# When the norm factors, the last sums of squares and two weight chunks are taken in a hybrid encoder trunk

## The chip, the cores and the metric

The kernel runs on one core of a Trainium2 chip. The metric is device time in microseconds (us), the median of several runs; lower is better. A core has TensorE (PE; its weight loads are PEld), VectorE (DVE), ScalarE (ACT), GpSimd (POOL) and SyncE (SP), which issues most DMAs. Each engine works through its own queue in order, and engines wait for one another at semaphores.

## The reference

Two layers on a sequence of 1024 positions of width 1024, all in float32. Cut to what matters:

```python
def rms_norm(x, g):
    y = x * rsqrt(mean(x * x, axis=-1) + 1e-6)
    return y * g

for layer in range(2):
    if layer == 0:
        x = x + ab_mixer(rms_norm(x, ab_norm), ...)   # mLSTM heads and gated MLP groups
    else:
        x = x + mla_mixer(rms_norm(x, c_norm), ...)   # attention from low-rank latents
    hf = rms_norm(x, ffn_norm[layer])
    x = x + square(relu(hf @ ffn_w1[layer])) @ ffn_w2[layer]   # width 4096 inside
return rms_norm(x, final_norm)
```

`mla_mixer` first projects the normed x to a key-value latent of 256 rows, a rotary key and a query latent of 384 rows, and norms both latents.

## The kernel before

Activations lie feature by feature, 128 features on the partitions and 1024 positions along the columns. Each product is made of three: a float32 operand is split into a high part (a ScalarE cast, `hi`, `wo`, `whi`) and a low part (the rest, a subtraction, mostly on VectorE: `lo`, `wlo`), and high x high, high x low and low x high are added up in PSUM. The norm's gain is multiplied in ahead of a product; the norm's factor, one number for each position, is multiplied in behind it. A factor is made in three moves: `rstd_sums` (L519) puts the sums of squares of a position on TensorE, sixteen small matmuls; `rstd_from` (L526) makes the root of it with twelve small VectorE operations; `spread_parts` (L549) builds two diagonal tiles `dg` on VectorE, and `spread_sums` (L567) lets TensorE spread them over the partitions, four matmuls, which ScalarE copies to `rb`.

**The MLP, first half** (`strassen_up`, L627). The product is done by Strassen's scheme: 16 quads q of output tiles, seven products each, so steps g = 7q + s. A product is 12 matmuls of 512 columns into one of four kinds of PSUM bank, A to D, with two banks each. The order of TensorE, VectorE and ScalarE is written out by hand in the loop over g: after the product of step g come, in this order, the weights' parts of step g+3 (`up.parts`), the sum of weights of step g+4 (`up.combine`), loads, relu and square of the results, a sum of the second product's weights (`sums.step`, stored to HBM), and the evacuation of the bank (`evacuate`). The norm's sums stand behind product 3, the factor in step 4, `dg` in step 5, the spread behind product 6; with it `relu` (L696, which multiplies `rb` in) of quad 0 in step 7 and its squares and stores in step 8. For later quads relu stands in the evacuation itself.

**The MLP, second half** (`strassen_down`, L756). Seven passes of eight steps (n = 8 pi + kp, the pass's product is i = DOWN[pi]); a step is 24 matmuls. In each step `fetch` (L395) starts the next weight chunk: a load by SP into one of two buffers `raw`, the cast on ScalarE, the low part on VectorE; `weights` (L415) takes the oldest one out. So a step works on a chunk that was fetched one step earlier. `di.parts(n + 2)` splits the activations two steps ahead. The last pass of the last layer (i = 2) keeps its first six weight chunks in tiles of their own (`khi`, `klo`), as it goes over the columns in quarters: eight steps with 24 matmuls of 256 columns, then the rest. In the pass before it (i = 4) the final norm of the other half is made: `Tail.step` (L294) adds up squares, then takes the sums in step 5, the spread in step 6 and in step 7 the output, eight products on POOL, each followed by a store of SP. SP's and POOL's order is the planner's, by its own estimates.

**Between the layers.** In the last pass of the first MLP `finish` (`next_norm`, L861) splits the new x for the attention block, squares it on ScalarE and adds the squares on POOL (`sq_add`, L506), four tiles in the pass and four (m = 0 to 3) behind it. The attention block's first products (`latent`, L1502) take k = 4 to 7 of two tiles first, then k = 0 to 3 of each. `later(n, fn)` (L453) runs `fn` on the n-th `tick`, and a tick stands behind each group of matmuls of one k: six of them in the latents, four in the key product. `x_col` (the sums and the factor) is set at tick 10, `x_spread` five ticks on, and the sums of the key-value latent follow in the same list. In this block only TensorE's order is written by hand.

Tiles of 1024 columns in SBUF come from 45 slots, given out first in, first out (`slot`, L347, `drop`, L353).

Of the kernel before, what the change touches and what calls it, by code (L numbers as in the profile page):

```python
# [18 lines left out]
D = 1024  # L19
T = 1024  # L20
NK = D // P
NC = T // P
# [287 lines left out]
class Kern:  # L310
# [316 lines left out]
    def strassen_up(self, layer, X, ss, hd, di):  # L627
        nc, tc = self.nc, self.tc
        self.pst.close()
        pool = self.pst.enter_context(tc.tile_pool(name=f"pu{layer}", bufs=2, space=PSUM, reuse_waits="tile"))  # L630
        bank = lambda t: pool.tile([P, 512], F32, tag=t, name=self.uid(t))
        self.bank = lambda: bank("A")
        up = self.up
        W = up.W
        N = 7 * NQ
        order = ((1, "A"), (5, "C"), (6, "B"), (7, "D"), (2, "A"), (3, "C"), (4, "D"))
        quads = {}
        sums = DownSums(self, layer)

        def product(g, ks=range(NK // 2), last=True):  # L640
            q, s = divmod(g, 7)
            i, b = order[s]
            first = s < 4
            if s == 0 and 0 in ks:
                quads[q] = {}
            if first and 0 in ks:
                quads[q][b] = bank(b)
            ps, w = quads[q][b], W[g]
            for kk in ks:
                o = X[i][kk]  # L650
                wh, wl = w[:, kk * P:(kk + 1) * P], w[:, H5 + kk * P:H5 + (kk + 1) * P]
                xh, xl = o[:, :H5], o[:, H5:2 * H5]
                for j, (a, x) in enumerate(((wh, xh), (wh, xl), (wl, xh))):

                    nc.tensor.matmul(ps, lhsT=a, rhs=x, start=first and kk == 0 and j == 0,  # L655
                                     stop=last and kk == NK // 2 - 1 and j == 2, skip_group_check=not first)
            if last:
                up.done(g)
                if q == NQ - 1:
                    self.drop(*X[i])  # L660

        rb, col, dg = [None], [None], []


        def evacuate(g):
            q, s = divmod(g, 7)
            t = quads[q]
            if s == 0:
                t["u"] = self.slot(name="u")
                nc.scalar.copy(out=t["u"][:, :H5], in_=t["A"])  # L670
                return
            if s == 1:
                return
            u = t["u"]
            if s == 2:
                nc.vector.tensor_tensor(out=u[:, H5:T], in0=t["B"], in1=u[:, :H5], op=ALU.add)
                nc.vector.tensor_tensor(out=u[:, :H5], in0=t["C"], in1=u[:, H5:T], op=ALU.add)
            elif s == 3:
                t["c1"] = self.slot(name="c1")
                nc.vector.tensor_tensor(out=t["c1"][:, H5:T], in0=t["D"], in1=u[:, :H5], op=ALU.add)  # L680
            elif s == 4:
                t["c0"] = self.slot(name="c0")
                nc.scalar.copy(out=t["c0"][:, :H5], in_=t["A"])
            elif s == 5:
                nc.vector.tensor_tensor(out=t["c0"][:, H5:T], in0=t["C"], in1=u[:, H5:T], op=ALU.add)
                if q > 0:
                    relu(q, 0)
                else:
                    dg[:] = self.spread_parts(col[0], NC, True)
            elif s == 6:  # L690
                nc.vector.tensor_tensor(out=t["c1"][:, :H5], in0=t["D"], in1=u[:, H5:T], op=ALU.add)
                self.drop(u)
                if q > 0:
                    relu(q, 1)

        def relu(q, i):  # L696
            c = quads[q][f"c{i}"]
            nc.vector.scalar_tensor_tensor(out=c, in0=c, scalar=0.0, in1=rb[0], op0=ALU.max, op1=ALU.mult)

        def square(q, i):  # L700
            c = quads[q].pop(f"c{i}")
            nc.scalar.activation(c, c, AF.Square)
            nc.sync.dma_start(out=hd[q // 2][q % 2 * 2 + i], in_=c)
            self.drop(c)

        with tc.manual_schedule(engines={mybir.EngineType.PE, mybir.EngineType.DVE, mybir.EngineType.Activation}):
            up.load(1)
            sums.load(0)

            for g in range(4):  # L710
                product(g, range(NK // 2 - 1), last=False)
            for g in range(N):
                q, s = divmod(g, 7)
                if g < 4:
                    product(g, (NK // 2 - 1,))
                else:
                    product(g)
                if g == 3:
                    ps = self.bank()
                    self.rstd_sums(ps, ss["ss"])  # L720
                    self.drop(ss["ss"])
                if g == 6:
                    rb[0] = self.spread_sums(dg, NC, True, [bank("B"), bank("C")])
                up.parts(g + 3)
                up.combine(g + 4)
                if s == 4:
                    up.load(q + 2)
                if g > 7 and s == 0:
                    square(q - 1, 1)
                elif s == 6 and q > 0:  # L730
                    square(q, 0)
                elif g == 7:
                    relu(0, 0)
                    relu(0, 1)
                elif g == 8:
                    square(0, 0)
                    square(0, 1)
                if g == 4:
                    col[0] = self.rstd_from(ps, D, "rc0")
                if q == NQ - 1:  # L740

                    if s < 4:
                        di.load(s)
                    if s in (2, 4):
                        di.parts(s // 2 - 1)
                    if s == 5:
                        self.fetch()
                sums.step(g)
                evacuate(g)
            square(NQ - 1, 1)  # L750
        self.drop(rb[0])
# [4 lines left out]
    def strassen_down(self, layer, di, spill, finish):  # L756
# [5 lines left out]
        last = layer == 1  # L762
        x = [None] * NK
# [35 lines left out]
        with tc.manual_schedule(engines={mybir.EngineType.PE, mybir.EngineType.DVE, mybir.EngineType.Activation}):  # L799
            for n in range(steps):  # L800
                pi, kp = divmod(n, NKP)
                i = DOWN[pi]
# [15 lines left out]
                    products(n, w, o, z, new)  # L818
                if not (last and i == 2):
                    di.done(n)  # L820
                di.load(n + 4)
                if n < NP:
                    for m in (n, n + NP):
# [37 lines left out]
    def next_norm(self, goff, xh, xl, state, spill):  # L861
        def finish(x, m):
            xh[m], xl[m] = self.split(x[m], g=self.cst[:, goff + m:goff + m + 1])
            state["ss"] = self.sq_add(state.get("ss"), x[m], eng=self.nc.gpsimd)
            self.nc.sync.dma_start(out=spill[m], in_=x[m])
            self.drop(x[m])
        return finish
# [614 lines left out]
    def mla(self, xh, xl, ss, source, spill):  # L1482
# [45 lines left out]
            nc.gpsimd.tensor_tensor(out=cs, in0=cs, in1=rxb, op=ALU.mult)  # L1528
            self.drop(rxb)

        self.later(10, x_col)
        self.later(5, x_spread)
        kvh, kvl, kvs = latent(KVL, C_KVG)

# [397 lines left out]
```

## Time and profile before

| | |
|---|---|
| runs, us | 2487.20, 2482.21, 2484.16 (median 2484.16) |
| the profiled execution's own time, us | 2484.26 |
| its span, us | 2482.6 |
| TensorE matmuls busy, us | 2405.1 (97%) |
| VectorE busy, us | 1773.4 (71%) |
| ScalarE busy, us | 1159.5 (47%) |
| GpSimd busy, us | 576.3 (23%) |
| chain that ended last | TensorE 87%, VectorE 7%, DMA 3% |

The span runs from the first to the last instruction; 1.7 us of the execution's time lie around it. Matmuls overlap: one of 512 columns is shown with some 0.39 us, while the next starts 0.23 us later. So a stretch of TensorE is measured from start to start. In windows, PEclk is the share of the full clock that TensorE was granted.

### The profile page before, as it was taken

How to read it: one execution, taken by the hardware profiler on the slowest of the kernel's cores; microseconds unless marked ns; L12 is line 12 of the kernel's file. 1: busy time of each engine (PE TensorE's matmuls, PEld its weight loads, DVE VectorE, ACT ScalarE, POOL GpSimd, SP SyncE). 2: the span in 40 equal slices, each digit the busy share in tenths (PEclk: the TensorE clock that was granted, in tenths of full speed). 3: DMA queues.
4: the chain of work that ended last, by engine and by line, in shares of the span. 5: the costliest groups of instructions: out<-in, count | busy, mean ns of one | idle time of the engine just before them, and what ended most of it. 6: DMA issues, size and time to landing. Idle time of an engine off the chain costs nothing.

```text
span 2482.6 us, 31418 instructions
## 1 busy us (share of the span) xinstructions
PE 2405.1 (97%) x11947; PEld 1999.9 (81%) x11947; DVE 1773.4 (71%) x2504; ACT 1159.5 (47%) x1717; POOL 576.3 (23%) x362
## 2 busy tenths in 40 slices
PE   7999989999999999999999999998999999999997
PEld 5788877778887788887788888887878888788887
DVE  6765487777777676664788888887577777667665
ACT  3354444433333333353567677677443333333353
POOL 4233344200000000024545454546310000000023
PEclk9999999999999999999999999999999999999999
DMA  3211113365568634351000000002346655953432
GB/s 116 69 60 63 49 48 115 139 229 203 217 221 298 213 110 153 108 172 39 22 18 22 18 19 17 13 26 94 119 146 235 226 207 215 341 162 97 160 109 96
DMA packets 96631, 309.49 MB, mean 125 GB/s; under 512 B 9984, under 2 KB 12992, under 8 KB 96480
## 3 DMA queue, kind: packets, MB, share of 16 engines
q1 hardware_dynamic: 95296, 304.81, 35.1%
q10 hardware_dynamic: 1152, 2.62, 0.3%
q8 instruction: 94, 1.54, 0.3%
q14 instruction: 57, 0.47, 0.1%
q0 software_dynamic: 32, 0.05, 0.0%
HBM read 219.53 MB, written 87.92 MB: 124 GB/s over the span
## 4 chain that ended last, share of the span: by engine, by line
PE 87%; DVE 7%; DMA 3%; ACT 1%; issue 1%; POOL 1%; DVEq 0%; ACTq 0%; POOLq 0%; SPq 0%
PE mm L432 18%; PE y L792 11%; PE z L792 11%; PE A L655 7%; PE C L655 6%; PE D L655 6%; PE s L1680 6%; PE po L1733 4%; PE pt L1714 4%; PE pj L432 4%; PE B L655 3%; DMA raw<-w 1%; DVE mx L1684 1%; DMA hq<-hd 1%; DVE nm L1686 1%
## 5 line engine op out<-in xcount | busy, mean ns | idle before, releaser
L411 ACT CAST whi<-raw 128x1024 fp32r<-128x1024 f32 x163 | 169.2, 1038 | 453.1 <-issue 226.5
L412 DVE TENSOR_TENSOR wlo<-raw,whi 128x1024 fp32r<-128x1024 f32 x110 | 138.6, 1260 | 208.9 <-ACT whi L411 204.8
L432 PE MATMUL mm<-hi,wlo 128*128 128x512 f32 x680 | 218.1, 399 | 2.6 <-POOL wlo L412 2.5
L432 PE MATMUL mm<-hi,whi 128*128 128x512 f32 x680 | 218.4, 399 | 0.0
L432 PE MATMUL mm<-lo,whi 128*128 128x512 f32 x680 | 218.3, 399 | 0.0
L1699 POOL TENSOR_SCALAR pr<-pr,rs 128x1024 f32<-128x1024 f32 x128 | 144.4, 1128 | 242.7 <-DVE rs L1698 203.2
L655 PE MATMUL A<-xo,wo 128*128 128x512 f32 x768 | 190.8, 397 | 1.4 <-DVE x L885 1.4
L655 PE MATMUL D<-xo,wo 128*128 128x512 f32 x768 | 188.8, 394 | 0.0
L1684 DVE TENSOR_REDUCE mx<-s 128x1 f32<-128x1024 f32 x128 | 155.6, 1216 | 46.5 <-PE s L1680 45.8
L655 PE MATMUL C<-xo,wo 128*128 128x512 f32 x768 | 188.6, 394 | 0.0
L412 POOL TENSOR_TENSOR wlo<-raw,whi 128x1024 fp32r<-128x1024 f32 (+1 forms) x53 | 131.2, 2477 | 244.4 <-ACT whi L411 208.1
L792 PE MATMUL y<-hi,wlo 128*128 128x512 f32 (+1 forms) x464 | 180.7, 389 | 2.5 <-DVE wlo L412 2.5
L792 PE MATMUL y<-hi,whi 128*128 128x512 f32 (+1 forms) x464 | 180.8, 390 | 0.0
L1692 ACT ACTIVATE pr<-s,nm,rqs 128x1024 f32<-128x1024 f32 x128 | 154.7, 1209 | 55.1 <-DVE nm L1686 53.2
L792 PE MATMUL y<-lo,whi 128*128 128x512 f32 (+1 forms) x464 | 180.3, 389 | 0.0
L655 PEld LDWEIGHTS A<-xo,wo 128*128 128x128 f32 x768 | 146.1, 191 | 35.5 <-issue 1.8
L1716 ACT CAST pth<-pt 128x512 fp32r<-128x512 f32 x256 | 138.2, 589 | 77.2 <-PE pt L1714 76.6
L655 PEld LDWEIGHTS D<-xo,wo 128*128 128x128 f32 x768 | 144.3, 188 | 33.9
L655 PEld LDWEIGHTS C<-xo,wo 128*128 128x128 f32 x768 | 144.0, 188 | 34.0 <-issue 0.4
L1718 DVE TENSOR_TENSOR ptl<-pt,pth 128x512 fp32r<-128x512 f32 x256 | 163.7, 680 | 7.1 <-ACT pth L1716 6.2
L792 PE MATMUL z<-hi,whi 128*128 128x512 f32 (+1 forms) x400 | 155.9, 390 | 0.0
L792 PE MATMUL z<-hi,wlo 128*128 128x512 f32 (+1 forms) x400 | 155.1, 388 | 0.5 <-DVE wlo L412 0.5
(352 smaller groups left out, 5511.1 us busy)
## 6 DMA issues: line engine op xcount, KB each, us to landing
raw<-w SPq DMA_DIRECT2D x112, 512.0 KB, 4.3
w2q<-w SPq DMA_DIRECT2D x64, 512.0 KB, 5.2
sd<-w2q SPq DMA_DIRECT2D x64, 512.0 KB, 6.6
hd<-c SPq DMA_DIRECT2D x64, 512.0 KB, 2.9
hq<-hd SPq DMA_DIRECT2D x64, 512.0 KB, 4.6
raw<-sd SPq DMA_DIRECT2D x64, 512.0 KB, 3.6
raw<-w_in SPq DMA_DIRECT2D x24, 512.0 KB, 3.6
xs<-x SPq DMA_DIRECT2D x24, 512.0 KB, 3.2
```

The source lines that it names most:

```text
L411: nc.scalar.copy(out=hi[:, :cols], in_=raw[:, :cols])
L412: self.lo_engine.tensor_tensor(out=lo[:, :cols], in0=raw[:, :cols], in1=f(hi[:, :cols]), op=ALU.subtract)
L432: nc.tensor.matmul(ps[:m, o:o + c], lhsT=w, rhs=x[:, t:t + c], start=k == first and i == 0, stop=k == (n - 1 if last is None else last) an ...
L655: nc.tensor.matmul(ps, lhsT=a, rhs=x, start=first and kk == 0 and j == 0, stop=last and kk == NK // 2 - 1 and j == 2, skip_group_check=not ...
L792: nc.tensor.matmul(Z[z, p][:, :c], lhsT=l[:, m], rhs=r[:, k], start=new and kp == 0 and kk == 0 and j == 0, stop=kp == NKP - 1 and kk == 1 ...
L1680: nc.tensor.matmul(ps[:, hsl], lhsT=lhs[:, qs], rhs=rhs[:, hsl], start=a, stop=z)
L1684: nc.vector.reduce_max(out=mx, in_=ps, axis=AX.X)
L1692: nc.scalar.activation(pr, ps, AF.Exp, bias=nm, scale=r["qs"][:, qb:qb + 1], accum_out=su)
L1699: nc.gpsimd.tensor_scalar(out=pr, in0=pr, scalar1=rs, scalar2=1.0, op0=ALU.mult, op1=ALU.mult)
L1714: nc.tensor.transpose(pt[:, j * P:(j + 1) * P], pr[:, c * P:(c + 1) * P], self.ident)
L1716: nc.scalar.copy(out=pth[half][:, :, qo], in_=pvs[half])
L1718: nc.vector.tensor_tensor(out=ptl[half][:, :, qo], in0=pv, in1=f(pth[half][:, :, qo]), op=ALU.subtract)
```

## The change

In the MLP's first half the factor moves from step 4 to step 8, `dg` from the evacuation of step 5 to step 9, the spread from behind product 6 to behind product 11, the two relus of quad 0 from step 7 to 12, and their squares and stores from step 8 to 13. The last two of these are no longer in one chain of conditions with quad 1's own square. Between the layers the four additions of squares behind the last pass go to VectorE instead of POOL, and the sums of the attention block's norm move from tick 10 to tick 14. In the pass before the last one, steps 5 and 6 start one more weight chunk each, behind their products.

```diff
@@ evacuate, s == 5
                 if q > 0:
                     relu(q, 0)
-                else:
-                    dg[:] = self.spread_parts(col[0], NC, True)
@@ strassen_up, the loop over g
-                if g == 6:
+                if g == 11:
                     rb[0] = self.spread_sums(dg, NC, True, [bank("B"), bank("C")])
                 up.parts(g + 3)
                 up.combine(g + 4)
...
                 elif s == 6 and q > 0:
                     square(q, 0)
-                elif g == 7:
+                elif g == 8:
+                    col[0] = self.rstd_from(ps, D, "rc0")
+                elif g == 9:
+                    dg[:] = self.spread_parts(col[0], NC, True)
+                elif g == 12:
                     relu(0, 0)
                     relu(0, 1)
-                elif g == 8:
+                if g == 13:
                     square(0, 0)
                     square(0, 1)
-                if g == 4:
-                    col[0] = self.rstd_from(ps, D, "rc0")
@@ strassen_down
                 if not (last and i == 2):
                     di.done(n)
+                if last and i == 4 and kp in (5, 6):
+                    self.fetch()
                 di.load(n + 4)
@@ next_norm, finish
-            state["ss"] = self.sq_add(state.get("ss"), x[m], eng=self.nc.gpsimd)
+            state["ss"] = self.sq_add(state.get("ss"), x[m],
+                                      eng=self.nc.vector if m < NK // 2 else self.nc.gpsimd)
@@ mla
-        self.later(10, x_col)
+        self.later(14, x_col)
         self.later(5, x_spread)
```

## Rows read from the trace of the kernel before

**Rows 1.** Waits of TensorE: total us, how often, longest us.

```profile
PE B L574 <- DVE dg L561: 7.3, 4, 3.2
PE pt L522 <- POOL ss L514: 4.2, 1, 4.2
PE y L792 <- DVE klo L412: 3.8, 4, 1.4
```

**Rows 2.** Timeline of TensorE, first MLP: start us, us, instructions [idle before].

```profile
492.14 2.94 PE L655 MATMUL D<-xo,wo 128*128 128x512 f32 x12
498.26 0.80 PE L574 MATMUL B<-dg,ones_r 128*128 128x512 f32 x1 [3.18 <-DVE dg L561]
...
500.84 4.70 PE L655 MATMUL A<-xo,wo 128*128 128x512 f32 x12
505.38 0.86 PE L655 MATMUL C<-xo,wo 128*128 128x512 f32 x3
```

**Rows 3.** The same of the second MLP.

```profile
1845.78 2.94 PE L655 MATMUL D<-xo,wo 128*128 128x512 f32 x12
...
1858.11 2.94 PE L655 MATMUL C<-xo,wo 128*128 128x512 f32 x12
```

**Rows 4.** Windows: length, busy us of PE, PEld, DVE, ACT, POOL, PEclk, DMA, GB/s.

```profile
498.30:505.40 7.10, 6.76 (x17) 4.96 (x18) 4.09 (x6) 2.31 (x4) 0.00 (x0) 0.55 0.42 148
505.40:560.00 54.60, 54.60 (x237) 44.30 (x236) 42.40 (x57) 21.21 (x32) 0.00 (x0) 1.00 0.63 232
...
1123.90:1139.20 15.30, 15.26 (x57) 12.87 (x58) 5.90 (x17) 4.40 (x6) 3.53 (x3) 0.71 0.10 35
...
2416.70:2445.50 28.80, 24.46 (x193) 23.00 (x193) 24.96 (x19) 16.23 (x20) 17.76 (x9) 1.00 0.48 163
```

**Rows 5.** Timeline of VectorE, first MLP, first operation of step 4.

```profile
490.27 0.68 DVE L599 TENSOR_TENSOR wo<-raw,wo 128x512 fp32r<-128x512 f32 x1
```

**Rows 6.** Timeline of TensorE, start of the attention block.

```profile
1105.78 0.62 PE L432 MATMUL mm<-hi,whi 128*128 128x512 f32 x2
...
1123.94 3.57 PE L522 MATMUL pt<-ones,ss 128*128 128x2 f32 x16 [4.17 <-POOL ss L514]
...
1137.81 0.62 PE L432 MATMUL mm<-hi,whi 128*128 128x512 f32 x2
```

**Rows 7.** Timeline of POOL, start of the attention block and last pass.

```profile
1110.93 12.96 POOL L514 TENSOR_TENSOR ss<-ss,sq 128x1024 f32<-128x1024 f32 x4 [15.16 <-ACT sq L513]
...
2412.11 16.95 POOL L289 TENSOR_TENSOR x<-x,rb 128x512 f32<-128x512 f32 x8 [14.63 <-ACT rb L576]
```

**Rows 8.** Timeline of VectorE, start of the attention block.

```profile
1110.36 1.28 DVE L498 SCALAR_TENSOR_TENSOR lo<-x,cst,hi 128x1024 fp32r<-128x1024 f32 x1
1111.87 9.82 DVE L498 SCALAR_TENSOR_TENSOR lo<-x,cst,hi 128x1024 fp32r<-128x1024 f32 x3 [0.23 <-ACT hi L497]
1127.55 0.17 DVE L531 TENSOR_SCALAR rv<-pt 128x8 f32<-128x8 f32 x1 [5.86 <-PE pt L522]
...
1131.39 1.22 DVE L561 TENSOR_TENSOR dg<-ident,cl 128x1024 fp32r<-128x1024 f32 x1
```

**Rows 9.** Timeline of VectorE around the start of the last pass.

```profile
2404.96 0.16 DVE L531 TENSOR_SCALAR rv<-y 128x4 f32<-128x4 f32 x1 [1.64 <-PE y L522]
...
2407.94 1.22 DVE L412 TENSOR_TENSOR wlo<-raw,whi 128x1024 fp32r<-128x1024 f32 x1
...
2413.01 1.47 DVE L412 TENSOR_TENSOR klo<-raw,khi 128x1024 fp32r<-128x1024 f32 x1 [2.72 <-ACT khi L411]
2414.41 2.32 DVE L502 TENSOR_TENSOR lo<-hq,hi 128x1024 fp32r<-128x1024 f32 x1
```

**Rows 10.** The page's DMA issues: KB each, median us to landing.

```profile
raw<-w SPq DMA_DIRECT2D x112, 512.0 KB, 4.3
w2q<-w SPq DMA_DIRECT2D x64, 512.0 KB, 5.2
sd<-w2q SPq DMA_DIRECT2D x64, 512.0 KB, 6.6
```

## The prediction

> **What bounds the kernel now.** TensorE is busy almost throughout, so an edit is worth only what it takes from TensorE's idle time and from its time at the lower clock. I read the waits of TensorE first [rows 1]. Three of them lie where the change works: the spread of the MLP's norm factors waits for dg (L574, four waits in the two MLPs), the sums of the attention block's norm wait for ss (L522, one wait), and the last pass waits for klo (L792). The timeline then gives what each costs in all. The reader should not add up idle times but take start to start and subtract the matmuls in between: an undisturbed stretch runs 237 matmuls in 54.60 us, 0.2304 us each [rows 4].
>
> First MLP: from the start of product 6 to that of product 8 it is 492.14 to 505.38, 13.24 us, for 28 matmuls (two products of 12, four of the spread), which want 6.45 [rows 2]. 6.8 us are lost: a wait of 3.2 at the spread, and behind it the granted clock falls (0.55 in the stretch after, the level 1.2 GHz for most of it [rows 4]), so that product 7 alone takes 4.5. Second MLP: 1845.78 to 1858.11, 12.33 us, 5.9 lost [rows 3]. Attention block: from the first matmul to the one behind the spread, 1105.78 to 1137.81, 32.0 us, for 94 matmuls (21.7) and the sums (3.57 at the lower clock, so some 1.8): 8.6 lost, by a wait of 4.2 and a mean clock of 0.71 behind it [rows 4, 6]. Last pass: 28.8 us for 192 matmuls of half width, 22.1 at half of 0.2304: up to 6.7 lost, in many small waits at full clock [rows 4].
>
> **MLP norm factors, twice.** The factor from the sums moves from step 4 to 8, the two dg from step 5 to 9, the spread from 6 to 11, the two relus from 7 to 12, their squares and two stores from 8 to 13. No instruction is added or removed. The wait vanishes if the second dg is ready at the end of product 11. Due time: products 7 to 11 follow product 6 without a break, 492.14 + 6 x 2.765 = 508.7. Ready time: VectorE stands at 490.27 at the first operation of step 4 [rows 5]. From there to the second dg, in the new order, it has 12 operations of 512 columns (0.68 each, 8.2), two sums of the second weights and two dg of 1024 columns (1.22 each as in [rows 8], 4.9), the twelve small ones of the factor (as in the last pass, 2404.96 to 2407.94 with a half-width dg of 0.7: 2.3 [rows 9]) and two more small ones (0.4): 15.8 us, at 506.1. So 2.6 us in hand; ScalarE's casts, for which VectorE waits once or twice on the way, may take up to 2 of it. Behind the spread, ScalarE holds the cast for product 14 until rb is copied (about 510); that weight is due at 517, so it is covered. The relus put 2 x 1.22 us on VectorE in step 12, ahead of the sums of steps 12 and 13; the weights of products 15 and 16 stand among them and are due 5 us later. The two c tiles hold their slots five steps longer, so the next loads of second weights fall on slots whose store has just been issued, and SP waits for its landing before the loads; they are first used four products later. I cost all this at nothing; uncovered it is up to 3 us in each MLP. Taken: 6.8 + 5.9 = 12.7 us back, with the lower clock, as no wait is left that starts it. Bounds 7 and 12.7.
>
> **Attention block's sums.** POOL's last four additions end near 1123.9 (12.96 us, four from 1110.93 [rows 7]). The change gives them to VectorE, where the same shape takes 1.22 us (dg, [rows 8]), between its four lo, each behind ScalarE's square. Those take 9.82 us for three beside POOL, but 1.28 for the first one, which POOL did not meet [rows 8]. So lo and addition together want 4 x 2.5 = 10.0 us from 1110.36 on, until 1120.4, and xl comes earlier than before. The sums are also moved, from the 10th to the 14th group of six matmuls, 1105.78 + 84 x 0.2304 = 1125.1. So 4.7 us in hand; either edit alone nearly does it (VectorE's at the 10th group: 0.8 us of wait; POOL's at the 14th: 1.2 in hand). POOL has nothing else queued there. What is late next: the spread now follows the sums by two groups of six matmuls and three of four, 24 x 0.2304 = 5.5 us, where before it was 30. The chain from factor to second dg takes 1127.55 to 1132.61, 5.1 us [rows 8], and starts about 0.2 after the sums: it just fits, 0.3 us in hand. VectorE's order here is the planner's; an operation of 1.28 placed in between would cost 1.0. The product with the cosines then has to be through POOL (2.4 us) before the key product ends, five groups of four later; 4.6 us, also close, but only VectorE waits for it, ahead of work for the next sums. Taken: 8.6 back less 0.2. Bounds 6.6 (1.0 lost at each of the two) and 8.6.
>
> **Last pass.** Two more fetches, in steps 5 and 6 of the pass before. Each is a raw load on SP, a cast on ScalarE and a low part on VectorE, emitted before that step's own cast and low part of the activations. TensorE's step k of the last pass needs klo k and lo k. Before, VectorE's order is lo k+1 ahead of klo k; with two chunks more it is klo k+1 ahead of lo k. Counted up to step k it is 2k+3 conversions either way. So nothing is really further ahead; only an earlier start would help. Before, VectorE idles 2.72 us before klo 0, because its cast stands on ScalarE behind the copy of rb, which waits for the spread [rows 9]. After, the chain looks like this. The cast of the weights of step 7 waits for TensorE to leave the buffer, at about 2404.5 (the sums right behind are read at 2404.96 [rows 9]); 1.05 for it, 1.14 from start to start for its low part, 1.14 for lo of step 7 behind it, 3.0 for the factor's chain behind that: it ends near 2410.8 instead of 2407.9, 0.4 late for the spread, due 24 matmuls behind the sums, at 2410.4. Then klo 0 to 2412.0, klo 1, lo 0 to about 2414.7. klo 2 needs the raw buffer that klo 0 leaves: 2412.0 + 4.3 for the load [rows 10] + 1.05 for the cast, 2417.4. VectorE idles 2.7 us there instead, and lo 1 stands behind it: TensorE's step 1 starts near 2421.5 where it was due at 2419.5. By then five conversions are done, as many as before at 2421.2. From there both orders are VectorE's, with 2.3 us for a conversion that meets POOL's eight products [rows 7, 9]. On SP the two raw loads go ahead of the eight output stores, which wait for those products. Taken: 0.5 us lost. The trace has no such order; its ends are 6.7 gained (every wait gone) and 2.5 lost (one more raw load behind a store of the output that waits for POOL).
>
> Beside POOL a VectorE operation takes 3.3 or 2.3 us where it takes 1.28 or 1.22 alone [rows 8, 9]. The Trainium skill (SBUF — State Buffer, the passage on the shared port pair) calls it an exclusive lock, held for the whole instruction. By that rule two klo pulled out of POOL's stretch would each save a whole product of POOL's (2.1 us, an estimate from the 16.95 us of eight [rows 7]), and the last pass would gain some 4 us instead of losing 0.5. Against this stands that lo 0 and lo 1 move into the stretch in their place.
>
> **Sum.** Against the profiled execution's own 2484.26 us (span 2482.6, 1.7 around it; the median of the runs is 2484.16): 12.7 + 8.4 - 0.5 = 20.6 back, less 0.2 for small waits that I don't see: 2484.3 - 20.4 = 2463.9, **2464 us**. Where later pauses stay, their price can shift a little, since the same wait of 3.2 us cost 6.8 in one MLP and 5.9 in the other; 1 or 2 us either way.
>
> **Rivals.** (a) A wait moves instead of going. Place: the spread in step 11, or the one in the attention block. For it: 2.6 and 0.3 us in hand are little, and VectorE's waits for ScalarE are estimated. Against it: steps 6 to 8 now have less on VectorE than before, so it arrives there early. A wait of 1 to 3 us in each MLP, with some of the lower clock: 3 to 5 us each, 6 to 10 in all: 2470 to 2474. (b) The last pass does what its edit is for: 4 to 6.7 gained: 2457 to 2460. For it: VectorE's idle 2.72 us and the 1.1 us that each conversion loses beside POOL. Against: the count above, and two raw buffers. (c) The change doesn't do what it says: behind dg something else was due as late. Against: the weights of products 7 and 8 were ready before the wait ended. It would give 2478 to 2484. (d) Slower than before: the slots. In the MLPs the pool of slots is nearly used up; if the two held tiles shift its rotation for good, each load of second weights waits for a store to land, eight times in each MLP. It decides from the point where store and load together outlast the four products (11 us) to first use: 6.6 and 5.2 us to landing make 11.8 [rows 10]. Each time from there on at 1 us of wait and 1 to 2 of the lower clock, 16 x 2.5 = 40 us: 2504. Against: the rotation is first in, first out and after step 14 as deep as before.
>
> **Chances.** Forecast (2460 to 2468) 0.66, (a) 0.15, (b) 0.11, (c) 0.04, (d) 0.04. Eight in ten: from 2458, half of (b), to 2471, the cheaper half of (a). A measurement of this kernel tells about 0.2%, 5 us, from no change. Faster by more: 0.92; within: 0.04; slower: 0.04.
>
> **What would show it.** In the profile after: no wait of TensorE at L574 in the MLPs and none at L522 in the attention block, full clock through both stretches, 12 matmuls each 2.77 us; ss written by VectorE four times near 1111 to 1120, and lo there at 1.28. In the last pass waits for lo where there were waits for klo, and the stretch still 28 to 30 us. Wrong would be: a wait at L574 in step 11 (VectorE later than I count), a stretch of 23 to 25 us at the end (the count of conversions misled me), or a lower clock without a wait ahead of it.

## The result and the profile after

The changed kernel takes 2464.41 us (median of four runs, 2463.22 to 2465.94); the kernel before, on the same chip, 2483.18 (four runs). The ratio is 0.9928, 95% interval 0.9915 to 0.994. The profiled execution of after took 2465.53 us, its span is 2463.8: 18.75 us shorter than the span before (20.4 were forecast).

Cut into stretches, each from the start of one matmul to the start of another, the two profiled executions compare as follows (us). The end of a half is the start of its last matmul. The last column is what the prediction said of that stretch.

| stretch | before | after | change | predicted |
|---|---|---|---|---|
| start to product 6 of the first MLP | 492.14 | 492.90 | +0.8 | 0 |
| first MLP, product 6 to the end of its first half | 301.86 | 295.39 | -6.5 | -6.8 |
| its second half | 311.55 | 311.49 | -0.1 | 0 |
| attention block, up to the first scores | 92.44 | 86.32 | -6.1 | -8.4 |
| scores to product 6 of the second MLP | 647.79 | 647.46 | -0.3 | 0 |
| second MLP, product 6 to the end of its first half | 301.23 | 294.66 | -6.6 | -5.9 |
| its second half up to the last pass | 269.73 | 270.79 | +1.1 | 0 |
| last pass up to its last quarter | 28.77 | 27.71 | -1.1 | +0.5 |
| the rest | 37.04 | 37.08 | 0.0 | 0 |

The waits of TensorE over the whole kernel (total us, how often, longest) answer [rows 1]:

```profile
PE y L792 <- DVE lo L502: 3.8, 4, 1.3
PE y L574 <- DVE dg L561: 3.0, 1, 3.0
...
PE pt L574 <- DVE dg L561: 1.7, 2, 1.5
```

The four waits of the MLPs' spread and the one of the attention block's sums are gone. The last pass waits as long as before, for lo instead of klo. New are two waits of 1.7 us in all at the spreads of the attention block. (The 3.0 us of y belong to the final norm, as before.)

TensorE in the first MLP, then in the second (start, us, matmuls), answering [rows 2, 3]:

```profile
492.90 2.94 PE L655 MATMUL D<-xo,wo 128*128 128x512 f32 x12
...
498.43 2.94 PE L655 MATMUL C<-xo,wo 128*128 128x512 f32 x12
...
509.57 0.62 PE L574 MATMUL B<-dg,ones_r 128*128 128x512 f32 x2
```

```profile
1833.56 2.94 PE L655 MATMUL D<-xo,wo 128*128 128x512 f32 x12
...
1839.11 2.92 PE L655 MATMUL C<-xo,wo 128*128 128x512 f32 x12
...
1850.18 0.63 PE L574 MATMUL B<-dg,ones_r 128*128 128x512 f32 x2
```

Product 6 to product 8 takes 5.53 and 5.55 us, two products of 12 matmuls; the spread behind product 11 waits for nothing. VectorE ends the second dg of the first MLP at 507.66, 1.9 us ahead of the spread's turn at 509.57:

```profile
506.44 1.22 DVE L561 TENSOR_TENSOR dg<-ident,cl 128x1024 fp32r<-128x1024 f32 x1
```

Windows over both MLPs' products 6 to 11, the attention block's sums and spread, and the last pass (length, busy us of PE, PEld, DVE, ACT, POOL, PEclk, DMA, GB/s), answering [rows 4]:

```profile
492.90:509.57 16.67, 16.67 (x73) 13.52 (x72) 14.88 (x31) 3.71 (x7) 0.00 (x0) 1.00 0.56 198
1833.56:1850.20 16.64, 16.64 (x74) 13.54 (x73) 14.83 (x31) 3.71 (x7) 0.00 (x0) 1.00 0.56 196
1115.00:1132.00 17.00, 15.52 (x76) 12.64 (x76) 10.10 (x19) 7.16 (x8) 7.25 (x4) 1.00 0.18 63
2399.01:2426.72 27.71, 23.93 (x194) 23.11 (x192) 23.78 (x18) 16.77 (x21) 18.07 (x9) 1.00 0.42 146
```

PEclk is 1.00 where it was 0.55 and 0.71: all these stretches run at 2.4 GHz. TensorE, VectorE and POOL at the start of the attention block, answering [rows 6 to 8]:

```profile
1119.42 1.84 PE L522 MATMUL pt<-ones,ss 128*128 128x2 f32 x16
...
1126.74 0.39 PE L574 MATMUL pt<-dg,ones_r 128*128 128x512 f32 x1
1128.61 0.96 PE L574 MATMUL pt<-dg,ones_r 128*128 128x512 f32 x3 [1.48 <-DVE dg L561]
```

```profile
1104.59 1.28 DVE L498 SCALAR_TENSOR_TENSOR lo<-x,cst,hi 128x1024 fp32r<-128x1024 f32 x1
1105.79 1.22 DVE L514 TENSOR_TENSOR ss<-ss,sq 128x1024 f32<-128x1024 f32 x1
...
1112.78 1.23 DVE L514 TENSOR_TENSOR ss<-ss,sq 128x1024 f32<-128x1024 f32 x1
...
1124.01 1.22 DVE L561 TENSOR_TENSOR dg<-ident,ch 128x1024 fp32r<-128x1024 f32 x1
1125.14 3.41 DVE L561 TENSOR_TENSOR dg<-ident,cl 128x1024 fp32r<-128x1024 f32 x1
```

```profile
1124.94 2.53 POOL L412 TENSOR_TENSOR wlo<-raw,whi 128x1024 fp32r<-128x1024 f32 x1 [4.29 <-issue]
```

The four lo and the four additions alternate on VectorE at 1.28 and 1.22 us, and the sums find ss ready 5.4 us early. But the second dg takes 3.41 us: POOL had begun a low part of the weights 0.2 us before it, and it ends 1.1 us behind that. That is the spread's new wait. In the kernel before, POOL stood idle behind its additions until 0.6 us after the second dg was through (1132.61 [rows 8]), so nothing met it; POOL's next operation there:

```profile
1133.19 2.40 POOL L412 TENSOR_TENSOR wlo<-raw,whi 128x1024 fp32r<-128x1024 f32 x1 [9.30 <-ACT whi L411]
```

VectorE and POOL at the start of the last pass, answering [rows 7, 9]:

```profile
2392.44 2.35 DVE L412 TENSOR_TENSOR klo<-raw,khi 128x1024 fp32r<-128x1024 f32 x2
2394.71 1.22 DVE L502 TENSOR_TENSOR lo<-hq,hi 128x1024 fp32r<-128x1024 f32 x1
2398.70 1.97 DVE L412 TENSOR_TENSOR klo<-raw,khi 128x1024 fp32r<-128x1024 f32 x1 [2.77 <-ACT khi L411]
2400.59 2.31 DVE L502 TENSOR_TENSOR lo<-hq,hi 128x1024 fp32r<-128x1024 f32 x1
...
2407.30 0.68 DVE L773 TENSOR_TENSOR x<-x,z 128x512 f32<-128x512 f32 x1
```

```profile
2394.70 16.07 POOL L289 TENSOR_TENSOR x<-x,rb 128x512 f32<-128x512 f32 x8 [15.10 <-ACT rb L576]
```

VectorE's idle 2.7 us have moved from the first klo to the third, as the prediction said, and beside POOL's eight products each conversion still takes up to 2.3 us.

### The profile page after: what moved, and what is told of

Its sections match the earlier page's. It is cut to its first block, busy times and chain, and to the rows that moved or that the text cites. A ratio compares the mean times of both kernels' runs of the same rounds, so it can differ in the third digit from the quotient of the medians.

```text
span 2463.8 us, 31412 instructions
## 1 busy us (share of the span) xinstructions
PE 2397.0 (97%) x11947; PEld 1992.9 (81%) x11947; DVE 1774.1 (72%) x2508; ACT 1158.9 (47%) x1717; POOL 564.8 (23%) x358
## 4 chain that ended last, share of the span: by engine, by line
PE 86%; DVE 8%; DMA 3%; issue 1%; ACT 1%; POOL 0%; DVEq 0%; ACTq 0%; POOLq 0%; SPq 0%
PE mm L432 17%; PE y L792 12%; PE z L792 11%; PE A L655 7%; PE C L655 7%; PE D L655 7%; PE s L1683 6%; PE po L1736 4%; PE pt L1717 4%; PE pj L432 4%; PE B L655 4%; DMA raw<-w 1%; DVE mx L1687 1%; DMA hq<-hd 1%; DVE nm L1689 1%
```

## The experiments

Below the row of after, mlp_only to vec_only share a chip and the runs of the kernel before (median 2483.56 us), so do the next four (tick_only to parts_first, 2482.44), then three (2484.16) and the last (2483.86). So medians of different groups can differ by some 1 us for that alone. Times are medians with lowest and highest; the last two columns are stretches of the profiled execution, as in the table above (attention block, last pass).

| kernel | us | ratio to before, interval | attention | last pass |
|---|---|---|---|---|
| after | 2464.41 (2463.22 to 2465.94) | 0.9928 (0.9915 to 0.994) | 86.32 | 27.71 |
| mlp_only | 2472.68 (2471.27 to 2474.42) | 0.9949 (0.9934 to 0.9963) | 92.49 | 28.63 |
| att_only | 2478.65 (2476.97 to 2479.54) | 0.9976 (0.9966 to 0.9987) | 86.15 | 28.66 |
| chunks_only | 2482.90 (2478.58 to 2485.04) | 0.9994 (0.9985 to 1.0004) | 92.33 | 29.21 |
| vec_only | 2478.13 (2474.82 to 2478.72) | 0.9970 (0.9957 to 0.9983) | 85.81 | 28.61 |
| tick_only | 2479.13 (2473.57 to 2483.79) | 0.9985 (0.9975 to 0.9994) | 86.51 | 28.59 |
| spread_7 | 2469.26 (2467.53 to 2470.76) | 0.9947 (0.9932 to 0.9962) | 91.06 | 27.71 |
| raw_slots | 2466.57 (2465.29 to 2467.01) | 0.9935 (0.9921 to 0.995) | 86.32 | 29.45 |
| parts_first | 2462.80 (2461.63 to 2464.18) | 0.9919 (0.9903 to 0.9936) | 86.28 | 26.89 |
| sums_12 | 2460.07 (2459.85 to 2460.59) | 0.9906 (0.9892 to 0.9921) | 84.58 | 28.11 |
| vec_out | 2459.61 (2458.45 to 2460.61) | 0.9904 (0.9889 to 0.9919) | 86.26 | 23.02 |
| vec_out_raw | 2460.39 (2458.87 to 2461.56) | 0.9907 (0.9891 to 0.9924) | 86.31 | 22.66 |
| sums_12_vec_out | 2459.72 (2454.32 to 2461.84) | 0.9899 (0.9885 to 0.9912) | 84.51 | 22.83 |

### The three parts, one by one

**mlp_only**: the kernel before with the edits in `strassen_up` alone.

```diff
-                if g == 6:
+                if g == 11:
                     rb[0] = self.spread_sums(dg, NC, True, [bank("B"), bank("C")])
...
+                elif g == 8:
+                    col[0] = self.rstd_from(ps, D, "rc0")
```

> The kernel before with the MLP part of the change alone. Theory: the pause at the spread and the lower clock behind it are all there is, so both MLPs run through product 6 to 8 in 5.5 us where they took 13.2 and 12.3, 12.5 to 13 us less in all. Rival: part of it goes back at later places (VectorE busy around step 12, the rotation of slots); then 6 to 10 us less, and the stretch from product 8 to the end of the first half grows.

Measured: both MLPs run through products 6 to 8 in 5.5 us. Product 6 to the end of the first half takes 295.37 us in the first MLP and 295.74 in the second, 6.5 and 5.5 less than before, 12.0 in all; the whole change has 295.39 and 294.66. The span is 12.9 us shorter (2469.6 against 2482.6) and the median 10.9. So the mechanism is the one of the theory; the size is at least 0.5 us under what it said.

**att_only**: the additions on VectorE and the sums at tick 14.

```diff
+            state["ss"] = self.sq_add(state.get("ss"), x[m],
+                                      eng=self.nc.vector if m < NK // 2 else self.nc.gpsimd)
...
-        self.later(10, x_col)
+        self.later(14, x_col)
```

> The kernel before with the attention block's part alone: the four additions on VectorE and the sums at tick 14. Theory: the wait of 4.2 us and the lower clock go, and a wait of 1.5 to 1.7 us stands at the spread, because the second dg meets POOL's low part of a weight chunk; 6 to 7 us less. Rival: the wait at the spread belongs to the order that the planner happened to choose beside the other parts; then it is absent here and 8 to 8.6 us go.

Measured: the block is 6.3 us shorter, as the theory says, not 8.4, and the spread waits 1.5 us in the changed kernel's manner. The median is 4.9 us lower.

**chunks_only**: the two fetches.

```diff
+                if last and i == 4 and kp in (5, 6):
+                    self.fetch()
```

> The kernel before with the two fetches alone. Theory: VectorE has the same number of conversions to do ahead of each step of the last pass, and the raw buffers hold the third chunk back, so nothing changes: within 1.5 us, the waits of TensorE in the last pass being for lo and no longer for klo. Rival: the fetches are worth 3 to 6 us and the profile of the whole change hides it in a loss elsewhere in the second MLP.

Measured: no difference that the time shows (interval 0.9985 to 1.0004); the last pass is 0.4 us longer.

By their spans the three parts give 12.9, 4.8 and 0.8 us, 18.5 together, where the whole change gives 18.75. That the sum is so close is luck: the start up to product 6 of the first MLP, which no part edits, is itself 1.6 and 1.4 us shorter than before in mlp_only and chunks_only and 1.6 longer in att_only. In the stretches that they work on the parts give 12.0, 6.3 and -0.4 us, 17.9 together, and the whole change 20.2 (more in the second MLP and in the last pass, see below). So they add up within some 2 us.

### What the attention block's gain needs

**vec_only**: the additions on VectorE, the sums left at tick 10.

```diff
+                                      eng=self.nc.vector if m < NK // 2 else self.nc.gpsimd)
```

> The kernel before with the four additions on VectorE, the sums left at tick 10. Theory: lo and additions end 14.0 us after the block's first matmul, the sums are due after 60 matmuls, 13.8 us: a wait of 0 to 0.8 us, no lower clock, and 30 matmuls then stand between sums and spread, so that the spread waits less than 0.5 us: 7.5 to 8.4 us less, more than with the move to tick 14. Rival: a wait at the sums of over 2 us, with the lower clock behind it: 3 to 6 us less.

**tick_only**: the sums at tick 14, the additions left on POOL.

```diff
-        self.later(10, x_col)
+        self.later(14, x_col)
```

> The kernel before with one edit: the attention block's sums stand at the 14th tick instead of the 10th; POOL still makes the four additions. Theory (from the prediction: either edit alone nearly does it): POOL ends its additions near 18.1 us after the block's first matmul, the sums are due 19.3 us after it, so TensorE doesn't wait there; lo beside POOL still takes 3.27 us each; what is late is the spread, by 0.3 to 1.6 us. 6 to 7.5 us less than the kernel before, 2476 to 2478. Rival: POOL comes later than that, because VectorE's lo and its additions hold each other up; then 1 to 4 us of wait stay at the sums, and the time is 2479 to 2483.

Measured: either alone gives 5.9 to 6.6 us in the block, as much as both (6.1 to 6.3). The medians fall by less, 5.4 us in vec_only and 3.3 in tick_only, so that the time of tick_only, 2479.1, lies in its rival's range, while its block shows the theory: no wait at the sums. In tick_only POOL is through 1.6 us ahead of the sums (additions from 1112.10, 13.03 us; sums at 1126.70), where the prediction had 1.2, and the second dg meets POOL's low part again. POOL and VectorE of tick_only:

```profile
1112.10 13.03 POOL L514 TENSOR_TENSOR ss<-ss,sq 128x1024 f32<-128x1024 f32 x4 [15.15 <-ACT sq L513]
...
1132.22 2.54 POOL L412 TENSOR_TENSOR wlo<-raw,whi 128x1024 fp32r<-128x1024 f32 x1 [4.07 <-issue]
```

```profile
1132.42 3.42 DVE L561 TENSOR_TENSOR dg<-ident,cl 128x1024 fp32r<-128x1024 f32 x1
```

In vec_only the sums start only 0.2 us late and the spread doesn't wait, since it is not near; but the granted clock falls behind the sums, so the 7.5 to 8.4 us of the theory are missed. Its windows:

```profile
1114.50:1121.40 6.90, 6.85 (x39) 5.59 (x38) 4.81 (x6) 1.47 (x2) 0.00 (x0) 1.00 0.15 60
1121.40:1124.80 3.40, 3.40 (x10) 2.63 (x8) 3.00 (x13) 0.00 (x0) 0.00 (x0) 0.50 0.00 0
```

Eight matmuls start in the 3.4 us at half the clock (the x10 counts those that reach in from outside); at full clock they want 1.8 (0.2304 each [rows 4]). So 1.6 us go there, as much as the spread's wait costs the others.

**spread_7**: the changed kernel with the spread two ticks later.

```diff
-        self.later(5, x_spread)
+        self.later(7, x_spread)
```

> The changed kernel with one edit: the spread of the attention block's factor stands seven ticks behind the sums instead of five, 32 matmuls (7.4 us) instead of 24 (5.5 us). Theory (the second dg, 3.41 us beside POOL's low part instead of 1.22, makes the spread wait): 5.1 us of the chain and 2.2 us of the longer dg fit into 7.4 us, the spread waits under 0.3 us, the time falls by 1.5 us against the changed kernel, to 2463. Rival: the wait moves, since the product with the cosines and the key's spread come two ticks later and the next factor stands behind them; then a wait of 1 to 2 us shows at the next spread and the time stays at 2464 to 2465.

Measured: 4.9 us slower than after; the rival holds, at a higher price than it named. The first spread no longer waits, but all behind it in the list comes later too, and the key-value factor falls among POOL's operations. VectorE, POOL and TensorE there:

```profile
1144.79 2.35 DVE L486 SCALAR_TENSOR_TENSOR ry<-rw,ry 128x8 f32<-128x8 f32 x1
...
1147.37 2.29 DVE L555 CAST ch<-rkv 128x8 fp32r<-128x8 f32 x1
1149.69 2.24 DVE L556 TENSOR_TENSOR cl<-rkv,ch 128x8 f32<-128x8 f32 x1
```

```profile
1144.67 4.94 POOL L502 TENSOR_TENSOR Kl<-kr,Kh 64x1024 fp32r<-64x1024 f32 x2 [9.02 <-issue]
1149.58 2.33 POOL L412 TENSOR_TENSOR wlo<-raw,whi 128x1024 fp32r<-128x1024 f32 x1
```

```profile
1153.13 0.79 PE L574 MATMUL pt<-dg,ones_r 128*128 128x512 f32 x1 [3.27 <-DVE dg L561]
```

Three operations on 8 columns, 0.17 us elsewhere, take 2.2 to 2.4 each, every one beside an operation of POOL, and a wait of 3.3 follows, with the lower clock behind it (0.51 from 1153.1 to 1160).

**sums_12**: the changed kernel with the sums two ticks earlier and the spread where it was.

```diff
-        self.later(14, x_col)
-        self.later(5, x_spread)
+        self.later(12, x_col)
+        self.later(7, x_spread)
```

> The changed kernel with one edit: the attention block's sums stand at the 12th tick instead of the 14th and the spread seven ticks behind them instead of five, so the spread and all that follows it keep their places. VectorE's last addition ends 5.4 us before the sums in the changed kernel, and the two ticks are 2.8 us, so the sums still don't wait. Theory (the spread's 1.5 us are only the chain from sums to second dg being too long for five ticks): that chain gets 2.8 us more, the spread waits under 0.3 us, and the key-value spread behind it stays as it was; 1.5 us less than the changed kernel, 2463. Rival: dg meets another operation of POOL or waits elsewhere; then 1 us or more stays, and the time is 2464 to 2465.

Measured: the block falls to 84.58 us, 7.9 less than before and 1.7 less than after; the time is 4.3 us below that of after. VectorE, then TensorE:

```profile
1123.54 1.22 DVE L561 TENSOR_TENSOR dg<-ident,cl 128x1024 fp32r<-128x1024 f32 x1
```

```profile
1126.53 1.08 PE L574 MATMUL pt<-dg,ones_r 128*128 128x512 f32 x4
```

The second dg is through as POOL's low part starts (1124.74), so it takes 1.22 us and nothing waits there. Of the 4.9 us that its span is shorter only 1.7 lie in this block; 3.3 lie behind it, between the scores and the second MLP, where the profiled execution kept the full clock around 1690 to 1730 (below; after had 0.91 there). So by its edit this kernel is worth 1.7 us.

### What sets the last pass

**raw_slots**: the changed kernel with the kept chunks loaded into slots of their own.

```diff
+        own = keep and len(self.wsrc) < NKP
+        raw = self.slot(name="raw") if own else self.wp.tile([P, 1024], F32, tag="raw", name=self.uid("raw"))
...
+        if own:
+            self.drop(raw)
```

> The changed kernel with one edit: the weight chunks that the last pass keeps are loaded into slots of their own instead of the two raw buffers, so no load waits for the low part of an earlier chunk. Theory A (the raw buffers hold the last pass back, as the prediction has it): the idle 2.8 us of VectorE before the third klo go, steps 1 and 2 of the last pass start 1 to 2.5 us earlier, the stretch from its first matmul to its last quarter falls from 27.7 us to 25 to 26.5, and the time to 2462 to 2463. Theory B (VectorE's total of conversions sets it, whatever its order): the idle time goes but comes back as a wait further on; the stretch stays at 27 to 28 and the time at 2464 to 2465.

Measured: VectorE's idle time goes, and the stretch gets 1.7 us longer (29.45), so both theories miss it. The time is 2.2 us above that of after. VectorE, then POOL:

```profile
2394.44 2.32 DVE L505 TENSOR_TENSOR lo<-hq,hi 128x1024 fp32r<-128x1024 f32 x1
2396.68 2.31 DVE L413 TENSOR_TENSOR klo<-raw,khi 128x1024 fp32r<-128x1024 f32 x1
```

```profile
2394.14 17.21 POOL L289 TENSOR_TENSOR x<-x,rb 128x512 f32<-128x512 f32 x8 [14.79 <-ACT rb L579]
2411.59 1.99 POOL L266 TENSOR_TENSOR ss<-ss,sq 128x512 f32<-128x512 f32 x1 [0.24 <-ACT sq L265]
```

Now the conversions from 2394 on meet POOL. The idle 2.8 us of the changed kernel were not lost: POOL got through two products at 1.29 us each meanwhile. And as the casts come earlier, so do the squares, and POOL's additions of squares (2411.59) fall among the conversions too.

**parts_first**: the changed kernel with each fetch behind the low part of the activations.

```diff
-                self.fetch()
+                late = last and n >= NKP * 5 + 6
+                if not late:
+                    self.fetch()
...
-                if last and i == 4 and kp in (5, 6):
-                    self.fetch()
...
                 di.parts(n + 2)
+                if last and n == NKP * 5 + 5:
+                    self.fetch()
+                if late:
+                    self.fetch()
+                    if n == NKP * 5 + 6:
+                        self.fetch()
```

> The changed kernel with one edit: in the last pass each weight chunk is fetched behind the low part of the activations of the same step instead of ahead of it, so that 2k+2 conversions instead of 2k+3 stand up to what step k needs; as many chunks are fetched ahead. Theory A (the order of VectorE's conversions sets the last pass, as the prediction counts it): one conversion of 1.2 to 2.3 us less ahead of each of the first steps; the stretch falls from 27.7 to 25.5 to 26.5 us, the time to 2462 to 2463. Theory B (the total or the wait for the third raw load sets it): the waits change their names from lo to klo, the stretch stays at 27 to 28.5 and the time at 2464 to 2466.

Measured: the stretch is 26.89 us, 0.8 less, between the two theories; the order counts for a little. The time, 1.6 us below that of after, can't decide: 1.5 us less lie between the scores and the second MLP, where nothing was edited.

**vec_out**: the changed kernel with POOL's eight products made by VectorE in the last quarters.

```diff
             elif kp == 7:
-                self.out(H5, H5)
+                self.held = self.rb
...
+            nc.vector.tensor_tensor(out=self.x[m][:, H5:T], in0=self.x[m][:, H5:T], in1=self.held[:, :H5], op=ALU.mult)
...
+                    tail.pair(p)
                     add(p, 0, Z["z", p][:, :h], h, h)
```

> The changed kernel with one edit: the eight output products that POOL makes in the last pass are made by VectorE behind it, two ahead of each quarter's first sum. Theory A (VectorE and POOL hold each other up, so the last pass is set by the sum of their work): lo and klo of the last pass take 1.22 us each instead of 2.3, the stretch falls from 27.7 to 23 to 25 us, the time by 2.5 to 4.5 us less what 5.5 us of products on VectorE cost behind it (under 0.5 us): 2460 to 2462. Theory B (two raw buffers set it): the operations are short but VectorE stands idle for the same time longer; the stretch stays at 26.5 to 28 and the time at 2463.5 to 2465.

Measured: the stretch falls by 4.7 us to 23.02, the time by 4.8. VectorE, and the window over the stretch:

```profile
2397.18 1.23 DVE L420 TENSOR_TENSOR klo<-raw,khi 128x1024 fp32r<-128x1024 f32 x1 [2.56 <-ACT khi L419]
2398.32 1.22 DVE L510 TENSOR_TENSOR lo<-hq,hi 128x1024 fp32r<-128x1024 f32 x1
```

```profile
2397.71:2420.73 23.02, 23.00 (x194) 22.79 (x192) 18.10 (x18) 16.53 (x21) 6.23 (x3) 1.00 0.27 93
```

The conversions that met the products are back at 1.22 us, and TensorE is busy for 23.00 of 23.02 us, although VectorE still idles 2.56 us for the third klo. Theory A holds: VectorE's and POOL's work add up, and that sum set the last pass. The eight products cost 0.5 us in the last quarters (37.57 against 37.08), so the edit is worth 4.2; 1.5 us of its shorter span lie between the scores and the second MLP.

**vec_out_raw**: the same with slots of their own for the raw loads.

> The same with the kept weight chunks loaded into slots of their own, so that neither POOL's products nor the two raw buffers hold the last pass back. If both theories hold in part: the stretch falls to 22.2 to 23.5 us, near what 192 matmuls want, and the time to 2459 to 2461. If POOL alone holds it back: no different from the run with the products moved alone, within 0.5 us of the stretch. If neither does: 27 to 29 us, as with slots of their own alone.

Measured: 22.66 us, and no gain in time. With POOL's products the two raw buffers were no limit (raw_slots), and without them they are worth 0.4 us of the stretch at most.

### The two together

**sums_12_vec_out**: both edits that helped.

> The changed kernel with both edits that helped alone: the sums at the 12th tick with the spread seven behind, and the last pass's eight output products on VectorE behind it. Theory: the two lie in stretches of their own and add up. By the two stretches alone, 2.0 us in the attention block and 4.7 in the last pass, that gives 2457.5 to 2458; by the medians of the two runs (4.3 and 4.8 us less than the changed kernel, in which a fall of the clock less in the attention part is counted) 2455 to 2456. Rival: the 2.3 us beyond its own stretch that the first edit showed are a chance order of the planner and don't come back; then 2457 to 2459.

Measured: 2459.72 us, no better than either alone; the theory's times were missed, and the rival's by 0.7. Both stretches keep their gain (84.51 and 22.83), but the profiled execution loses 3.6 us between the scores and the second MLP against sums_12 (647.77 against 644.13). The windows show where; first sums_12, then both together:

```profile
1690.00:1730.00 40.00, 35.49 (x215) 29.91 (x214) 25.60 (x42) 21.79 (x38) 18.15 (x12) 1.00 0.17 53
```

```profile
1690.00:1730.00 40.00, 34.82 (x200) 29.67 (x199) 25.79 (x42) 22.17 (x38) 18.31 (x12) 0.91 0.16 53
```

ScalarE's, VectorE's and POOL's counts are the same, the granted clock isn't, and TensorE gets through 200 matmuls instead of 215. The five runs lie between 2454.3 and 2461.8 us, far wider than those of sums_12 (2459.9 to 2460.6). One profiled execution each can't say how often the clock falls there; that stays open. The medians of the last four kernels in the table are 4 to 5 us below that of after; the intervals of the ratios of the first three overlap that of after by 0.0004 to 0.0009, that of the last lies just below it.

## Why the prediction was right, and where not

**Total.** 2464 us were predicted, 2464.4 measured; against the profiled execution's own time 20.4 us were forecast to come back and 18.7 did. The largest terms, the MLPs, hold. That the total is so near is also luck: the attention block gave 2.3 us less than forecast and the stretches put at nothing lost 1.5, while the last pass gave 1.6 more; and the median of the runs lies 1.1 below the profiled execution.

**MLPs, right.** 12.7 us forecast, 13.0 measured over the two first halves (6.5 and 6.6), 12.0 in mlp_only (6.5 and 5.5). Both reasons are seen: no wait and PEclk 1.00. The second dg is through 1.9 us ahead of the spread, where 2.6 were counted. The reckoning start to start, with the matmuls subtracted, found the cost of the lower clock that the idle time of 3.2 us doesn't show. The second half of the second MLP is 1.1 us longer than before, but that is hardly a cost of these edits: no wait shows it, and TensorE keeps the full clock; its matmuls only follow one another at a slightly greater distance, in att_only too, which has none of the MLP's edits. Stretches of 220 us there in before, after and att_only:

```profile
2170.00:2390.00 220.00, 220.00 (x957) 179.31 (x956) 145.56 (x140) 85.68 (x91) 6.04 (x5) 1.00 0.42 136
2152.00:2372.00 220.00, 220.00 (x953) 178.76 (x953) 145.06 (x140) 85.55 (x91) 5.90 (x5) 1.00 0.42 135
2165.50:2385.50 220.00, 220.00 (x954) 178.80 (x953) 144.85 (x140) 85.90 (x91) 6.25 (x5) 1.00 0.43 135
```

Four matmuls less are 0.9 us (0.2304 each). In the same way the first half of the second MLP fits 1231 matmuls into 284 us in after and 1226 in mlp_only, so that about 1 us of its 6.6 is not the edit's. What sets the distance stays open.

**Attention block, mechanism right, one term mis-sized.** 8.4 us forecast, 6.1 measured. The sums don't wait, VectorE's operations take 1.28 and 1.22, and "either edit alone nearly does it" is what vec_only and tick_only show. The term that failed is "the spread ... just fits, 0.3 us in hand", with 0.2 us for a miss: its chain takes 7.3 us (1121.30 to 1128.56) instead of 5.1, as the second dg was priced at 1.22 us, the row of a moment in which POOL was idle, and it meets POOL's low part of a weight chunk. The prediction asked which VectorE operation might be put in between; it didn't ask what POOL does then. "POOL has nothing else queued there" holds while the additions run, but already in the kernel before a low part on POOL followed only 0.6 us behind the second dg. sums_12, which only takes the chain out of POOL's way, brings 7.9 of the 8.4 us.

**Last pass, right for the edit alone, and not in the whole change.** "0.5 us lost" was forecast. Alone (chunks_only) the edit loses 0.4 us; in the whole change the stretch takes 27.71 us (28 to 30 said), 1.1 less than before and 0.9 less than in mlp_only and att_only, where this edit is missing. Waits for lo in place of klo, idle VectorE ahead of the third klo, the spread 0.3 late: all there, in both. The two kernels part near the end of the stretch, where POOL adds up squares. POOL and VectorE in chunks_only, then VectorE and POOL in after:

```profile
2432.69 1.39 POOL L266 TENSOR_TENSOR ss<-ss,sq 128x512 f32<-128x512 f32 x1 [5.46 <-issue]
2432.83 2.33 DVE L502 TENSOR_TENSOR lo<-hq,hi 128x1024 fp32r<-128x1024 f32 x1
```

```profile
2416.37 1.21 DVE L502 TENSOR_TENSOR lo<-hq,hi 128x1024 fp32r<-128x1024 f32 x1
2416.75 1.99 POOL L266 TENSOR_TENSOR ss<-ss,sq 128x512 f32<-128x512 f32 x1 [5.99 <-issue]
```

Where the addition is first, lo is late: TensorE waits for lo 5.3 us in chunks_only and 3.8 in after, which is the 1.5 us between them. The forecast has no term for that order, which hangs on a few tenths of a us, so the gain in the whole change was not foreseen.

But the count of conversions and the two raw buffers are not what sets the pass: raw_slots takes the buffers away and is slower, parts_first takes a conversion away and gains 0.8. vec_out shows the real limit, VectorE and POOL in each other's way. So of the rival's 6.7 us 5.8 were there to be had (28.77 to 23.02), but not by fetching earlier alone. Whether POOL's products could have gone without the two fetches was not tried.

Beside POOL, lo and klo go at 2.31 us and x<-x,z, whose z lies in PSUM, at its usual 0.68. The Trainium skill (SBUF — State Buffer, "Who interferes with whom") says that a VectorE instruction with two inputs from SBUF contends with a GpSimd instruction that reads SBUF, and one with a single SBUF input doesn't unless it runs in a two-port mode. These rows agree. (The cast in spread_7, with one input, was held up too; the page's exception would cover it, but no run here tells.) The prediction cited that page's lock against the last pass; the place where it decided a term was the attention block, where it was not applied.

**Rivals.** (a), a wait that moves instead of going, came true for the attention block at 1.5 us, not for the MLPs. (b), (c) and (d) didn't occur: the last pass gained 1.1 us, not 4 to 6.7, and both first halves are shorter by 6.5 and 6.6 us.

## What to carry to other kernels

Price a stall by the distance from start to start less the matmuls in between, and the slack of what comes next by the chain that will then run, with each operation at the duration it has beside whatever POOL does at that moment. Where VectorE and GpSimd both have a queue of two-input operations, add up their times: here filling VectorE's idle time, reordering it or loading earlier changed the stretch by -0.8 to +1.7 us, and moving one engine's share out of it took 4.7 us away. And judge an edit by the stretch that it works on: elsewhere in the kernel the profiled executions differ by up to 5 us without any edit.

## What the runs showed of the hardware

- Next to a POOL operation the size of a VectorE operation hardly matters: in spread_7 three of 8 columns take 2.24 to 2.35 us, and one of 1024 columns in the changed kernel 3.41; none of them ended before the POOL operation beside it.
- The clock fell in vec_only behind a stretch in which TensorE was busy for 6.85 of 6.90 us, with a wait of 0.2 us ahead of the sums; in the changed kernel the same sums, without that wait, left it at 1.00.
- The same wait at the second MLP's spread cost differently from kernel to kernel: product 6 to product 8 takes 12.2 to 12.4 us in before, att_only, chunks_only and tick_only, and 13.65 in vec_only.
- Part of the gain or loss of an edit shows far from it: between the scores and the second MLP the kernels here take 644.1 to 648.9 us, though none of them changes anything there.
- At full clock and without a wait, matmuls of 512 columns do not follow one another at the same distance in every kernel: 957 in 220 us in before, 953 in after, in the same part of the second MLP.
